# A forward state-space sweep whose rows of prefix sums are requested a quarter earlier, whose two decay products share one tile, and a convolution whose tanh is emitted later

## The chip, the cores and the metric

The kernel runs on one core of one Trainium2 chip. The metric is the device time of one execution, in microseconds (us); the median of three runs before the change is 3792.83 us. The core's engines run side by side, each with its own queue worked off in order: TensorE (PE in the rows, its weight loads PEld), VectorE (DVE), ScalarE (ACT), GpSimd (POOL), and SyncE (SP), which here only issues DMAs.

## The reference

The program is a two-layer network over 256 context and 2048 latent tokens of width 1024, batch 1, float32. The change touches only the even layer's state-space group:

```python
xbc = silu(dwconv(xbc_raw, conv_w, conv_b))        # 5 taps, 1536 channels
xc    = x * dt                                     # 16 heads of 64, chunks of 128 tokens
acum  = cumsum(dt * a)                             # per head, along a chunk
decay = exp(where(lower, acum[l] - acum[s], NEG))  # 128 x 128 per head and direction
y_diag = einsum(C @ B^T, decay, xc)                # within a chunk
y_off  = einsum(C, h_prev, exp(acum))              # from the state before the chunk
```

It is done forwards and backwards over the tokens and both are added. 18 chunks (2 of context, 16 latent) by 16 heads are computed. Attention, gating, an S5 layer and a final norm follow, which the change leaves as they are.

## The kernel before

The even layer's input stage lasts from the start to about 1520 us. TensorE's main work there is the input projection: each weight block of 128 columns is multiplied with "chunks" of 256 tokens, 24 matmuls of 128x128 by 128x256 into one of two PSUM buffers `mm` (float32 split into a high and a low part, three products by eight slices of the contraction). Each filled `mm` must be copied out by ScalarE (or by ScalarE and VectorE together) before TensorE may fill it again. The rows of the sequence are cut into thirds of 768 tokens. For each third, one small block `dt` and 12 convolution blocks run; then the remaining blocks (gate z, q, k, v, g) run for the thirds 2, 1, 0.

A convolution block ends with `conv()`: ScalarE writes the first tap into `cA` (L611, one buffer), VectorE adds four taps in place (L614), ScalarE takes the tanh into `cT` (L617) and VectorE finishes the silu (L618). Twelve units of planned time later `tok()` transposes the block on TensorE (L629, PSUM buffers `tp`, two of them, also used by the dt transposes L804) and ScalarE copies it out (`cE`, L631).

Beside this a second stream, `stream2()`, makes the forward sweep: 18 chunks of 128 tokens by four "quarters" of four heads each. `ssd_fa` does the elementwise part of a quarter and `ssd_fb` its matmuls (`yd`, L964), two quarters behind. In `ssd_fa`, `rf` and `rb` are 128x512 tiles that hold four heads' prefix sums broadcast to all partitions, each loaded by one DMA (L934, L935), two buffers each. ScalarE adds the per-row sum (L942, four instructions), VectorE combines with `rb` (L946, four), ScalarE takes exp (L948). Beside it the product with the masked C B^T of the chunk: ScalarE writes `w1` (L943, four, one buffer) from `cL`, VectorE adds the `cU` part into `w2` (L947, four, three buffers), and L949 multiplies `w2` by `rf`, which is the last read of `rf`. In the rows both tiles are called `w`, since numbers are left out of names.

The code is emitted in an order set by planned time: `merge` steps the main stream, `after(t, f)` calls `f` once the planned clock has passed `t` units, and each quarter of the second stream takes its turn as its share of the budget allows. TensorE executes in just that order. The other engines' instructions, DMA issues of SP among them, are reordered by a scheduler that goes by its own estimates, and are then fixed queues. A tile whose buffer is still in use makes the first instruction that writes it wait.

Of the kernel before, what the change touches and what calls it, by code (L numbers as in the profile page):

```python
# [7 lines left out]
F32 = mybir.dt.float32  # L8
# [3 lines left out]
AF = mybir.ActivationFunctionType  # L12
ALU = mybir.AluOpType
# [3 lines left out]
P = 128  # L17
# [13 lines left out]
AH = 1  # L31
GLD = 16.0
HL = 5.0
RV, KV, QV = 4, 4, 4
GD = 5.0
WGS = 3
# [19 lines left out]
def dap(t, off, dims):  # L56
    return bass.AP(tensor=t.tensor, offset=t.offset + off, ap=[list(d) for d in dims])
# [175 lines left out]
class Net:  # L233
# [220 lines left out]
    def even_in(self):  # L454
        nc, i, tc = self.nc, self.i, self.tc
        with ExitStack() as st:
# [110 lines left out]
            s_dt, s_nP, s_de, s_yo, s_cd = [cp.tile([P, NT, 32], F32, name=n) for n in ("s_dt", "s_P", "s_de", "s_yo", "s_cd")]  # L567
            self.s_dt, self.s_P, self.s_de, self.s_yo, self.s_cd = s_dt, s_nP, s_de, s_yo, s_cd
            self.hst = {0: None, 1: None}

            pj = Proj(self, w_in, 5152, xp, wp, pp)
            thr = lambda th: range(3 * th, 3 * th + 3)
# [6 lines left out]
            def conv_block(th, b):  # L579
# [9 lines left out]
                n = sum(s[1] for s in segs)  # L589
# [15 lines left out]
                def conv():  # L605
# [3 lines left out]
                    acc = vp.tile([P, 896], F32, name="cA", bufs=1)  # L609
                    for (s, m, q) in segs:  # L610
                        nc.scalar.activation(acc[:, q:q + m], R[:, s:s + m], AF.Identity, bias=cbv[:, b:b + 1], scale=cw[:, b:b + 1])  # L611
                    for j in range(1, 5):
                        for (s, m, q) in segs:
                            nc.vector.scalar_tensor_tensor(acc[:, q:q + m], R[:, s + j:s + j + m], cw[:, 12 * j + b:12 * j + b + 1],  # L614
                                                           acc[:, q:q + m], op0=ALU.mult, op1=ALU.add)
                    tg = vq.tile([P, 896], F32, tag="cT", name="cT", bufs=2)
                    nc.scalar.activation(tg[:, :n], acc[:, :n], AF.Tanh)  # L617
                    nc.vector.scalar_tensor_tensor(tg[:, :n], tg[:, :n], 1.0, acc[:, :n], op0=ALU.add, op1=ALU.mult)  # L618
# [14 lines left out]
                        if b == 7:  # L633
                            self.done.add(("xbc", th))
                    if b < 10:
                        self.after(12.0, tok)
                return pj.feat(1024 + b * P, evac, conv, chunks=thr(th))

            def rest_blocks(th):
# [263 lines left out]
    def ssd_off(self, d, c, g, ct, out):  # L903
# [4 lines left out]
        nc.vector.tensor_tensor(out.rearrange("p (h q) -> p h q", h=8), ps.rearrange("p (h q) -> p h q", h=8),  # L908
                                self.s_yo[:, c, h0:h0 + 8][:, :, None].to_broadcast([P, 8, 64]), ALU.mult)

    def ssd_fa(self, c, qq, st):

        nc, sp, pp = self.nc, self.sp, self.pp
        V, G = nc.vector, nc.gpsimd
# [14 lines left out]
        cU, cL = st["c"]  # L929
        g, h0 = qq // 2, qq * 4  # L930
        sh = [P, 4, P]
        rf = sp.tile(sh, F32, name="rf", bufs=2)
        rb = sp.tile(sh, F32, name="rb", bufs=2)
        nc.sync.dma_start(rf, dap(self.prow_d, (c * 32 + h0) * P, [[0, P], [P, 4], [1, P]]))  # L934
        nc.sync.dma_start(rb, dap(self.prow_d, (c * 32 + 16 + h0) * P, [[0, P], [P, 4], [1, P]]))  # L935
        A = nc.scalar
        w1 = sp.tile(sh, F32, name="w1", bufs=1)
        w2 = sp.tile(sh, F32, name="w2", bufs=3)

        for h in range(4):  # L940
            hh = h0 + h
            A.activation(rf[:, h], rf[:, h], AF.Identity, bias=self.s_P[:, c, hh:hh + 1])  # L942
            A.activation(w1[:, h], cL[:, g], AF.Copy, scale=self.s_dt[:, c, 16 + hh:17 + hh])  # L943
        for h in range(4):
            hh = h0 + h
            V.scalar_tensor_tensor(rf[:, h], rb[:, h], self.s_P[:, c, 16 + hh:17 + hh], rf[:, h], op0=ALU.add, op1=ALU.min)  # L946
            V.scalar_tensor_tensor(w2[:, h], cU[:, g], self.s_dt[:, c, hh:hh + 1], w1[:, h], op0=ALU.mult, op1=ALU.add)  # L947
        A.activation(rf, rf, AF.Exp)  # L948
        V.tensor_tensor(w2, w2, rf, ALU.mult)  # L949
        st["w"][qq] = w2  # L950
# [85 lines left out]
    def attention(self):  # L1036
# [4 lines left out]
        with ExitStack() as st:  # L1041
# [268 lines left out]
            def half_proj():  # L1310
                for half in range(2):
# [20 lines left out]
                    if half == 0:  # L1332

                        for _ in range(4):
                            z = ada_load()
                            yield ("until", self.pe + HL)
                            ada_mm(z)
# [862 lines left out]
```

## Time and profile before

| what | value |
|---|---|
| median of 3 runs (lowest to highest) | 3792.83 us (3790.74 to 3793.8) |
| the profiled execution: its time, its span | 3789.91 us, 3788.1 us |
| TensorE busy | 3447.3 us, 91% of the span |
| VectorE, ScalarE, GpSimd busy | 2477.5 us (65%), 1614.5 us (43%), 1146.1 us (30%) |
| mean granted TensorE clock (1 is the full 2.4 GHz) | 0.959 |
| DMA queue 1, share of 16 engines | 63.5% |

TensorE's busy share counts matmuls that overlap in its pipeline; what the other engines cost shows up as idle time before a matmul, and as a lower granted clock after it. The clock has two levels, 2.4 GHz (1.0) and 1.2 GHz (0.5).

### The profile page before, as it was taken

Reading aid. Unit: us, or ns where it says so; the run is one execution under the profiler, and the core shown is the slowest. Engines: PE = TensorE matmul, PEld = TensorE weight load, DVE = VectorE, ACT = ScalarE, POOL = GpSimd, SP = SyncE. Lnnn points to the kernel's source line nnn. Section 1 sums busy time; section 2 is a strip of 40 time slices with the busy share of each in tenths; the row PEclk is TensorE's granted clock in tenths of the full one; section 3 lists DMA queues with packets and bytes.
Section 4 is the critical chain, followed back from the end, with each engine's and each line's share of the span. In section 5 each row is a group of like instructions: output and inputs, shape, how many; then the busy total and the mean of one; then the engine's idle time right before and its main releaser. Section 6 shows DMA issues by size and latency. Waiting matters only on the chain.

```text
span 3788.1 us, 68824 instructions
## 1 busy us (share of the span) xinstructions
PE 3447.3 (91%) x25733; PEld 3100.0 (82%) x25733; DVE 2477.5 (65%) x5414; ACT 1614.5 (43%) x3519; POOL 1146.1 (30%) x754
## 2 busy tenths in 40 slices
PE   6979999998999998789999998978899979989999
PEld 4978898987898888668878887757788978979977
DVE  5878876566535444867677776798893599504355
ACT  4545454443422222667677765222222522343321
POOL 3222234332222332366566652210101111133121
PEclk8989999999999999899999999989899999999999
DMA  8666568775666776675555444557877854895453
GB/s 287 219 212 197 176 216 267 251 233 194 218 233 207 261 253 211 188 195 148 147 138 136 117 115 131 163 171 230 256 239 244 295 185 147 272 299 163 126 167 112
DMA packets 668025, 759.33 MB, mean 200 GB/s; under 512 B 77147, under 2 KB 529691, under 8 KB 667691
## 3 DMA queue, kind: packets, MB, share of 16 engines
q1 hardware_dynamic: 667691, 754.93, 63.5%
q8 instruction: 203, 3.33, 0.4%
q14 instruction: 131, 1.07, 0.1%
HBM read 517.62 MB, written 237.15 MB: 199 GB/s over the span
## 4 chain that ended last, share of the span: by engine, by line
PE 30%; DVE 13%; DMA 7%; SPq 2%; issue 2%; ACT 2%; POOL 1%; DVEq 0%; ACTq 0%; POOLq 0%
PE pv L1184 3%; PE pt L1174 3%; PE S L1154 2%; PE mm L289 2%; PE gpo L291 2%; PE gpo L290 2%; PE gpo L289 2%; PE S L1156 2%; PE mm L290 2%; PE mm L291 2%; DVE sc L1896 1%; PE f L289 1%; PE f L291 1%; PE f L290 1%; DVE sc L1899 1%
## 5 line engine op out<-in xcount | busy, mean ns | idle before, releaser
L289 PE MATMUL mm<-xTh,wh 128*128 128x256 f32 (+1 forms) x3320 | 1014.8, 306 | 68.9 <-ACT cR L603 22.4
L290 PE MATMUL mm<-xTl,wh 128*128 128x256 f32 (+1 forms) x3320 | 956.6, 288 | 1.3 <-POOL xTl L274 0.7
L291 PE MATMUL mm<-xTh,wl 128*128 128x256 f32 (+1 forms) x3320 | 955.8, 288 | 0.5 <-DVE wl L274 0.5
L289 PEld LDWEIGHTS mm<-xTh,wh 128*128 128x128 f32 (+1 forms) x3320 | 648.6, 195 | 100.9 <-ACT cR L603 24.8
L290 PEld LDWEIGHTS mm<-xTl,wh 128*128 128x128 f32 (+1 forms) x3320 | 648.6, 195 | 18.2 <-issue 14.9
L291 PEld LDWEIGHTS mm<-xTh,wl 128*128 128x128 f32 (+1 forms) x3320 | 646.8, 195 | 1.7 <-DVE wl L274 0.8
L1178 DVE TENSOR_TENSOR tl<-pt,th 128x512 fp32r<-128x512 f32 x328 | 224.2, 687 | 117.6 <-ACT th L1177 115.1
L1167 DVE TENSOR_SCALAR_CACHE_REDUCE p<-S,nsink 128x640 f32<-128x640 f32 (+2 forms) x288 | 235.3, 820 | 79.4 <-PE S L1156 76.6
L1168 ACT ACTIVATE p<-p,nm 128x640 f32<-128x640 f32 (+2 forms) x288 | 223.9, 777 | 69.9 <-DVE p L1167 67.8
L1177 ACT ACTIVATE th<-pt 128x512 fp32r<-128x512 f32 x328 | 194.2, 593 | 132.0 <-PE pt L1174 128.6
L289 PE MATMUL mm<-wh,xTh 128*128 128x256 f32 x720 | 217.9, 303 | 20.0 <-DMA wh<-wk 10.6
L1174 PE MATMUL pt<-ident,p 128*128 128x128 f32 x1312 | 203.4, 277 | 33.4 <-ACT p L1168 14.2
L1174 PEld LDWEIGHTS pt<-ident,p 128*128 128x128 f32 x1312 | 156.1, 141 | 68.4 <-issue 18.7
L290 PE MATMUL mm<-wl,xTh 128*128 128x256 f32 x720 | 206.7, 287 | 1.7 <-POOL wl L274 1.0
L291 PE MATMUL mm<-wh,xTl 128*128 128x256 f32 x720 | 206.3, 287 | 0.0
L946 DVE SCALAR_TENSOR_TENSOR rf<-rb,s_P,rf 128x128 f32<-128x128 f32 x288 | 135.0, 514 | 97.8 <-ACT rf L942 92.1
L614 DVE SCALAR_TENSOR_TENSOR cA<-cR,vecs,cA 128x256 f32<-128x256 f32 (+3 forms) x192 | 182.6, 962 | 23.6 <-ACT cA L611 20.2
L401 POOL TENSOR_TENSOR xin<-xin,shr 128x1024 f32<-128x1024 f32 x33 | 86.3, 2625 | 313.3 <-issue 185.4
L289 PEld LDWEIGHTS mm<-wh,xTh 128*128 128x128 f32 x720 | 140.9, 196 | 27.6 <-DMA wh<-wk 11.4
L274 POOL TENSOR_TENSOR wl<-w,wh 128x1024 fp32r<-128x1024 f32 (+1 forms) x43 | 100.4, 2338 | 199.7 <-ACT wh L282 177.8
L576 ACT ACTIVATE tz<-mm 128x256 f32<-128x256 f32 x144 | 54.0, 378 | 232.4 <-PE mm L291 229.9
L408 PE MATMUL tp<-ident,xin 128*128 128x128 f32 x432 | 93.9, 304 | 63.7 <-DVE xTl L274 44.8
(458 smaller groups left out, 9011.7 us busy)
## 6 DMA issues: line engine op xcount, KB each, us to landing
wh<-wk SPq DMA_DIRECT2D x116, 512.0 KB
wl<-wk SPq DMA_DIRECT2D x116, 512.0 KB
wk<-wh SPq DMA_DIRECT2D x56, 512.0 KB
wk<-wl SPq DMA_DIRECT2D x56, 512.0 KB
w<-in_e_w_in_dram SPq DMA_DIRECT2D x40, 512.0 KB
xin<-in_x_dram SPq DMA_DIRECT2D x38, 512.0 KB
rf<-prow_d SPq DMA_DIRECT2D x72, 256.0 KB
rb<-prow_d SPq DMA_DIRECT2D x72, 256.0 KB
```

The source lines that it names most:

```text
L274: eng.tensor_tensor(out, x, hi.bitcast(F32), ALU.subtract)
L289: mm(ps, lhsT=ah, rhs=bh, start=first, stop=False)
L290: mm(ps, lhsT=ah, rhs=bl, start=False, stop=False)
L291: mm(ps, lhsT=al, rhs=bh, start=False, stop=last)
L614: nc.vector.scalar_tensor_tensor(acc[:, q:q + m], R[:, s + j:s + j + m], cw[:, 12 * j + b:12 * j + b + 1], acc[:, q:q + m], op0=ALU.mult, ...
L946: V.scalar_tensor_tensor(rf[:, h], rb[:, h], self.s_P[:, c, 16 + hh:17 + hh], rf[:, h], op0=ALU.add, op1=ALU.min)
L1167: V.tensor_scalar(p[:, :w], s, -0.125, nsink[:, h:h + 1], op0=ALU.mult, op1=ALU.min, accum_out=nm)
L1168: A.activation(p[:, :w], p[:, :w], AF.Exp, bias=nm, scale=-1.0, accum_out=d["sm"][:, h:h + 1])
L1174: T.transpose(pt[:, n, :], Ps[h4][:, j * P:(j + 1) * P], self.ident)
L1177: A.activation(th, pt, AF.Copy)
L1178: V.tensor_tensor(tl, pt, th.bitcast(F32), ALU.subtract)
L1184: T.matmul(pv, lhsT=VV[kt][:, hk, :], rhs=t.rearrange("p a b -> p (a b)"), start=first and x == 0, stop=last and x == 1)
```

## The change

Three edits. First, `ssd_rows` issues both row loads of a quarter; `ssd_fa` calls it for the next quarter at the start of the present one (not across the ends of the three thirds' sweeps, where it loads its own rows as before). The tiles keep two buffers. Second, `w1` is gone: ScalarE writes its product into `w2`, VectorE adds to it in place, and `w2` has four buffers in place of three. Third, tanh and all that follows of a convolution block are called `CVT` = 4 planned units after the taps; the transposes keep 12 units from the block's end in the text of the plan.

```diff
+CVT = 4.0
@@ conv() of conv_block
                             nc.vector.scalar_tensor_tensor(acc[:, q:q + m], R[:, s + j:s + j + m], cw[:, 12 * j + b:12 * j + b + 1],
                                                            acc[:, q:q + m], op0=ALU.mult, op1=ALU.add)
+                    self.after(CVT, lambda: silu(acc))
+
+                def silu(acc):
                     tg = vq.tile([P, 896], F32, tag="cT", name="cT", bufs=2)
...
                     if b < 10:
-                        self.after(12.0, tok)
+                        self.after(12.0 - CVT, tok)
@@ class Net
+    def ssd_rows(self, c, qq):
+
+        r = [self.sp.tile([P, 4, P], F32, name=n, bufs=2) for n in ("rf", "rb")]
+        for d in range(2):
+            self.nc.sync.dma_start(r[d], dap(self.prow_d, (c * 32 + 16 * d + qq * 4) * P, [[0, P], [P, 4], [1, P]]))
+        return r
@@ ssd_fa
-        rf = sp.tile(sh, F32, name="rf", bufs=2)
-        rb = sp.tile(sh, F32, name="rb", bufs=2)
-        nc.sync.dma_start(rf, dap(self.prow_d, (c * 32 + h0) * P, [[0, P], [P, 4], [1, P]]))
-        nc.sync.dma_start(rb, dap(self.prow_d, (c * 32 + 16 + h0) * P, [[0, P], [P, 4], [1, P]]))
+        rf, rb = self.rows_q.pop((c, qq), None) or self.ssd_rows(c, qq)
+        if (c, qq) not in ((4, 3), (10, 3), (17, 3)):
+
+            n = (c, qq + 1) if qq < 3 else (c + 1, 0)
+            self.rows_q[n] = self.ssd_rows(*n)
         A = nc.scalar
-        w1 = sp.tile(sh, F32, name="w1", bufs=1)
-        w2 = sp.tile(sh, F32, name="w2", bufs=3)
+        w2 = sp.tile(sh, F32, name="w2", bufs=4)
 
         for h in range(4):
             hh = h0 + h
             A.activation(rf[:, h], rf[:, h], AF.Identity, bias=self.s_P[:, c, hh:hh + 1])
-            A.activation(w1[:, h], cL[:, g], AF.Copy, scale=self.s_dt[:, c, 16 + hh:17 + hh])
+            A.activation(w2[:, h], cL[:, g], AF.Copy, scale=self.s_dt[:, c, 16 + hh:17 + hh])
         for h in range(4):
             hh = h0 + h
             V.scalar_tensor_tensor(rf[:, h], rb[:, h], self.s_P[:, c, 16 + hh:17 + hh], rf[:, h], op0=ALU.add, op1=ALU.min)
-            V.scalar_tensor_tensor(w2[:, h], cU[:, g], self.s_dt[:, c, hh:hh + 1], w1[:, h], op0=ALU.mult, op1=ALU.add)
+            V.scalar_tensor_tensor(w2[:, h], cU[:, g], self.s_dt[:, c, hh:hh + 1], w2[:, h], op0=ALU.mult, op1=ALU.add)
```

The order changes on all engines up to the end of the forward sweep and is the same behind it. Line numbers of the changed kernel are higher: L603, L611, L617, L631, L813, L942, L943, L948 become L605, L613, L622, L636, L818, L954, L955, L960, and both row loads stand in L920.

ScalarE at the first chunk of the second third's blocks, where the sweep's first products are made. `cR` are copies out of `mm`, `d_e` belongs to the dt block; the kernel before:

```order
L603 ACTIVATE cR<-mm 128x256
L943 ACTIVATE w_2423<-cL,s_dt 128x128 x4
L611 ACTIVATE cA<-cR,vecs 128x768
L813 ACTIVATE d_e<-d_e 128x192
L943 ACTIVATE w_2570<-cL,s_dt 128x128 x4
L603 ACTIVATE cR<-mm 128x256 x2
L942 ACTIVATE rf<-rf,s_P 128x128 x4
```

and the changed kernel:

```order
L605 ACTIVATE cR<-mm 128x256 x3
L636 ACTIVATE cE<-tp 128x512
L613 ACTIVATE cA<-cR,vecs 128x768
L636 ACTIVATE cE<-tp 128x128
L818 ACTIVATE d_e<-d_e 128x192
L955 ACTIVATE w_2453<-cL,s_dt 128x128 x4
L955 ACTIVATE w_2612<-cL,s_dt 128x128 x4
L955 ACTIVATE w_2814<-cL,s_dt 128x128 x4
L955 ACTIVATE w_2992<-cL,s_dt 128x128 x4
L605 ACTIVATE cR<-mm 128x256 x3
```

The products of all four quarters now stand in one piece behind `d_e` and ahead of the copies; before, those of the second quarter did, and the third and fourth came later.

ScalarE at the first chunk of the last third's blocks, again products, copies and the row lines; before:

```order
L943 ACTIVATE w_4099<-cL,s_dt 128x128 x4
L690 ACTIVATE dT<-mm 32x256
L943 ACTIVATE w_4338<-cL,s_dt 128x128 x4
L943 ACTIVATE w_4512<-cL,s_dt 128x128 x4
L603 ACTIVATE cR<-mm 128x256
L942 ACTIVATE rf<-rf,s_P 128x128 x8
L603 ACTIVATE cR<-mm 128x256
L948 ACTIVATE rf<-rf 128x512
L631 ACTIVATE cE<-tp 128x512
```

and the changed kernel:

```order
L955 ACTIVATE w_4121<-cL,s_dt 128x128 x4
L955 ACTIVATE w_4359<-cL,s_dt 128x128 x4
L955 ACTIVATE w_4532<-cL,s_dt 128x128 x4
L605 ACTIVATE cR<-mm 128x256
L954 ACTIVATE rf<-rf,s_P 128x128
L605 ACTIVATE cR<-mm 128x256
L954 ACTIVATE rf<-rf,s_P 128x128 x3
L818 ACTIVATE d_e<-d_e 128x192
L954 ACTIVATE rf<-rf,s_P 128x128 x4
L960 ACTIVATE rf<-rf 128x512
L605 ACTIVATE cR<-mm 128x256
L636 ACTIVATE cE<-tp 128x512
```

The products keep their place; the second copy moved ahead of three quarters of the row lines. On TensorE the dt transposes L804, which stood right behind a block's transposes L629, now stand one chunk of 24 matmuls ahead of them.

SP in the gate blocks of the second third, one chunk of the sweep; `wk` are weights read back for a later block, `xs`, `ct`, `bt` the sweep's other loads; before:

```order
L934 DMA rf<-prow_d 128x512 x2
L868 DMA xs<-xs_d 128x1024
L648 DMA z_d<-zt 128x2x256
L870 DMA ct<-ct_d 128x2x128
L872 DMA bt<-btok_d 128x256
L935 DMA rb<-prow_d 128x512 x2
L934 DMA rf<-prow_d 128x512
L976 DMA yp_d<-y 128x1024
L648 DMA z_d<-zt 128x2x256
L935 DMA rb<-prow_d 128x512
L934 DMA rf<-prow_d 128x512
L82 DMA wl<-wk_2720_01_7100 128x1024
```

and the changed kernel:

```order
L920 DMA rf<-prow_d 128x512 x2
L873 DMA xs<-xs_d 128x1024
L653 DMA z_d<-zt 128x2x256
L875 DMA ct<-ct_d 128x2x128
L877 DMA bt<-btok_d 128x256
L920 DMA rb<-prow_d 128x512
L988 DMA yp_d<-y 128x1024
L920 DMA rb<-prow_d 128x512
L920 DMA rf<-prow_d 128x512 x2
L653 DMA z_d<-zt 128x2x256
L920 DMA rb<-prow_d 128x512 x2
L83 DMA wh<-wk_2720_00_7075 128x1024
```

The four `rf` loads stand at the same count ahead of the weights, and one more `rb` does. Over the whole sweep no weight load has its count of `rf` or `rb` loads ahead of it changed by more than two of 72, and most by none.

## Rows read from the trace of the kernel before

**Rows 1.** Busy time by engine, 60 to 560 us; then granted clock, DMA share, GB/s

```profile
60.00:560.00 500.00, 447.12 (x3530) 429.12 (x3530) 414.69 (x639) 244.50 (x546) 139.26 (x91) 0.95 0.64 206
```

**Rows 2.** What TensorE waited for, 60 to 1120 us: total, times, longest

```profile
PE mm L289 <- ACT cR L603: 22.4, 8, 9.6
...
PE mm L289 <- DVE zt L577: 11.6, 7, 2.7
PE mm L289 <- DMA wh<-wk: 9.1, 2, 4.7
PE tp L804 <- ACT cE L631: 8.4, 2, 7.8
PE mm L289 <- DVE qev L577: 8.3, 3, 4.1
```

**Rows 3.** Groups by line, 60 to 1110 us: busy, mean ns | idle before, releasers

```profile
L943 ACT ACTIVATE w<-cL,s_dt 128x128 f32<-128x128 f32 x288 | 92.6, 391 | 77.2 <-DVE w L947 53.6 <-DVE cL L924 23.1
L942 ACT ACTIVATE rf<-rf,s_P 128x128 f32<-128x128 f32 x288 | 92.3, 391 | 109.3 <-DMA rf<-prow_d 108.7
...
L617 ACT ACTIVATE cT<-cA 128x640 f32<-128x640 f32 (+2 forms) x36 | 30.3, 843 | 52.2 <-DVE cA L614 48.3 <-DMA prow_d<-rows 4.0
...
L947 DVE SCALAR_TENSOR_TENSOR w<-cU,s_dt,w 128x128 f32<-128x128 f32 x288 | 113.9, 448 | 15.5 <-PE yd L964 9.2 <-ACT w L943 6.3
```

**Rows 4.** Timeline, 231 to 243 us: start, length, engine, line, [idle before, releaser]

```profile
231.55 0.35 ACT L813 ACTIVATE d_e<-d_e 128x192 f32<-128x192 f32 x1
...
233.19 1.91 POOL L926 TENSOR_TENSOR y<-xs,dskip 128x1024 f32<-128x1024 f32 x1
...
233.27 7.70 DVE L947 SCALAR_TENSOR_TENSOR w<-cU,s_dt,w 128x128 f32<-128x128 f32 x4
...
241.01 1.28 ACT L943 ACTIVATE w<-cL,s_dt 128x128 f32<-128x128 f32 x4 [9.11 <-DVE w L947]
...
242.60 0.58 PE L289 MATMUL mm<-xTh,wh 128*128 128x256 f32 x1 [9.59 <-ACT cR L603]
```

**Rows 5.** Timeline, 381 to 395 us, ScalarE and TensorE

```profile
381.31 1.28 ACT L943 ACTIVATE w<-cL,s_dt 128x128 f32<-128x128 f32 x4 [5.71 <-DVE cL L924]
...
385.89 0.82 PE L629 MATMUL tp<-ident,cT 128*128 128x128 f32 x6
...
388.94 0.36 ACT L603 ACTIVATE cR<-mm 128x256 f32<-128x256 f32 x1
389.71 1.28 ACT L942 ACTIVATE rf<-rf,s_P 128x128 f32<-128x128 f32 x4 [0.42 <-DMA rf<-prow_d]
391.93 1.28 ACT L942 ACTIVATE rf<-rf,s_P 128x128 f32<-128x128 f32 x4 [0.94 <-DMA rf<-prow_d]
...
394.53 0.84 PE L804 MATMUL tp<-ident,dT 32*128 32x32 f32 x6 [7.82 <-ACT cE L631]
```

**Rows 6.** Timeline, 95 to 97 us, ScalarE and TensorE

```profile
95.29 0.74 ACT L617 ACTIVATE cT<-cA 128x640 f32<-128x640 f32 x1 [11.05 <-DVE cA L614]
...
96.36 0.58 PE L289 MATMUL mm<-xTh,wh 128*128 128x256 f32 x1 [7.17 <-ACT cR L603]
```

**Rows 7.** Busy time and clock in three short stretches (columns as Rows 1)

```profile
242.00:245.60 3.60, 3.00 (x14) 3.00 (x15) 3.60 (x7) 1.42 (x5) 0.00 (x0) 0.50 0.24 73
245.60:249.20 3.60, 3.60 (x32) 3.60 (x32) 3.60 (x11) 2.49 (x9) 0.00 (x0) 1.00 0.28 71
...
389.00:399.20 10.20, 4.67 (x24) 4.61 (x25) 5.90 (x16) 5.27 (x16) 0.00 (x0) 0.50 0.40 120
```

**Rows 8.** Timeline, 821 to 827 us: a row buffer's last read, its load, its next use

```profile
821.61 1.41 DVE L949 TENSOR_TENSOR w<-w,rf 128x512 f32<-128x512 f32 x1
...
823.08 0.32 SPq L934 DMA_DIRECT2D rf<-prow_d  x1
...
826.52 1.28 ACT L942 ACTIVATE rf<-rf,s_P 128x128 f32<-128x128 f32 x4 [3.05 <-DMA rf<-prow_d]
```

**Rows 9.** What SP's queue waited for, 170 to 1110 us: total, times, longest

```profile
SPq L934 <- DVE w L949: 59.0, 36, 12.1
```

More of the change, by code (lines that the diff above doesn't have):

```diff
@@ L569, in even_in @@
             self.hst = {0: None, 1: None}
+            self.rows_q = {}
             pj = Proj(self, w_in, 5152, xp, wp, pp)
```

## The prediction

> **What bounds the kernel now.** I first read the order of before and after, which says where to look: only the stretch up to the end of the forward sweep changes, and TensorE's instructions there are the same ones. What can move the time is therefore TensorE's idle time in that stretch and the clock it loses by it. Busy time by stage shows TensorE at 447.12 of 500 us and VectorE not far behind at 414.69 [rows 1]. TensorE's waits say what ends its idle time: mostly a copy out of PSUM that comes late, by ScalarE (`cR` 22.4 us in 8 waits, `cE` 8.4) or by ScalarE and VectorE together (`zt` 11.6, `qev` 8.3), and twice a weight load (9.1) [rows 2]. Two of these waits are nearly half of it: 9.59 us at 242.6 and 7.82 us at 394.5; a third is 7.17 us at 96.4 [rows 4 to 6]. Why ScalarE is late then stands in its groups by line: it sits idle in front of the row lines for DMA (108.7 us), in front of the products for VectorE's use of the single `w1` (53.6 us), and in front of the tanh for the taps (48.3 us) [rows 3]. The three edits aim at one of these each. Idle time of ScalarE costs only where a copy that TensorE needs stands behind it, so I price the edits by TensorE's stalls.
>
> A stall also costs clock. After the 9.59 us the granted clock is 0.50 for 3.6 us, in which 14 matmuls pass; in the next 3.6 us, at 1.00, 32 do [rows 7]. So one matmul takes 3.6 / 32 = 0.1125 us at the full rate, a chunk of 24 takes 2.7 us, and work done at the low level costs half its time extra.
>
> **The products (`w1` gone, fourth buffer).** At 241.01 ScalarE starts the second quarter's products after 9.11 us of waiting for VectorE, whose four L947 took 7.70 us; the copies of `mm` stand behind, and TensorE waits 9.59 us [rows 4]. In the new order 16 products stand behind `d_e` and need no VectorE. `d_e` ends at 231.55 + 0.35 = 231.90. Four products take 1.28 us at 0.391 each, so a further one adds (1.28 - 0.39) / 3 = 0.297 us, and 16 take 0.39 + 15 x 0.297 = 4.8 us. The copy, 0.36 us, ends at about 237.1 in place of 242.6. TensorE had run dry at 242.60 - 9.59 = 233.0, so about 4.1 us of idle stays and 5.5 us go. The low clock stays as long as a wait of that size does; I count none back. Bounds: nothing, if `cL` or the taps hold the copies anyway, and 9.6 + 1.5 us if all of it goes.
>
> At 394.5 TensorE has been dry since 394.53 - 7.82 = 386.7. Twelve products from 381.31 on take 3.7 us, so the first copy comes at 385.0 in place of 388.94 [rows 5], and the dt transposes, which waited for a PSUM buffer of the transposes just ahead, stand a chunk earlier. TensorE gets one chunk, 2.7 us, to 389.4; the second copy then stands behind one row line, whose DMA lands at 389.71, and comes by 390.5 (1.1 us idle); the third stands behind the other row lines, 391.93 + 1.28, an exp and itself, about 394.2, against a chunk that ends at 393.2 (1.0 us idle). Of 7.8 us some 2.1 stay and 5.7 go, and of the 4.67 us of work at the low level [rows 7], which costs 2.3 us, I take half back: 6.9 us. Bounds 0 and 7.8 + 2.3 = 10.1.
>
> The fourth buffer ends VectorE's 9.2 us of waiting for `yd` before L947 [rows 3]. That reaches TensorE only where a `zt` or `qev` stands behind it: between 0 and 9.2 us, I take 1, since VectorE's other delays stay.
>
> **The tanh.** It is called two chunks later, but the queue's order shows that the scheduler had already put one or two `cR` copies ahead of it; now it is mostly two. At 95.3 the taps ended late (11.05 us of waiting), one copy more now stands ahead, and TensorE gets one more chunk before it is dry: 2.7 of 7.17 us [rows 6]. The other `cR` waits are 22.4 - 9.59 - 7.17 = 5.6 us together; I take 1. Bounds 0 and 7.2 + 5.6 + 2.9 us of clock. The transposes go one chunk later, and the code behind them has room: no TensorE wait in rows 2 is for a sweep load.
>
> **The rows a quarter ahead.** I take nothing, and this is the choice that decides the sum. ScalarE's 108.7 us look like loads asked for too late. But a row load waits for its buffer and not for its turn: at 821.61 + 1.41 = 823.02 the last read of an `rf` buffer ends, at 823.08 SP issues the load of the quarter two later into it, and 3.4 us after that ScalarE uses it, having waited 3.05 [rows 8]. SP waited for that reader 36 times, 59.0 us [rows 9]. The queue already runs ahead as far as two buffers let it; the change keeps two buffers, and the order of SP shows the loads at almost the same count among the weight loads. Bounds: the stalls a late row can have held, `zt` and `qev`, 11.6 + 8.3 = 19.9 us saved; and 9.1 us lost if the one `rb` more ahead of some weight loads makes the two waits for weights as long again.
>
> **The sum.** 5.5 + 6.9 + 1 + 2.7 + 1 + 0 = 17.1 us. TensorE's gained time brings work to VectorE faster, and that is 83% busy in the convolution stage (414.69 of 500); I give 3 us back for stalls that come up elsewhere. That leaves 14 us: the profiled execution, 3789.91 us, would take 3776, and the median, which lies 2.9 us above it, 3792.83 - 14 = 3779.
>
> **Rivals.**
>
> *The early rows do help.* For it: 108.7 us of DMA waiting is the largest sum on ScalarE. Against it: rows 8 and 9. It would add most of the 19.9 us: about 3779 - 18 = 3761. 13%.
>
> *VectorE takes the place of the wait.* Without ScalarE's wait the four L947 still take 7.70 us, where four at the mean of 0.448 would take 1.8; GpSimd's multiplies of 1.9 us run beside them [rows 3, 4]. Everything behind them, taps, exp's inputs, `zt`, is as late as before, and with `cA` in one buffer the copies of `cR` soon wait for the taps. Then only the 2.7 us of the tanh stay: about 3790, range 3785 to 3797. For it speaks the 83%, against it that VectorE also idles in front of these lines. 27%. The Trainium skill, page "SBUF — State Buffer", section "SBUF: two separate sides", has a rule for the long L947: a VectorE operation with two SBUF inputs and a GpSimd operation that reads SBUF take a shared port pair as an exclusive lock for a whole instruction. By that rule the in-place add, which still has two SBUF inputs, is held as before, and this rival's time would hold; the trace agrees as to the length (7.70 us beside 1.91 us multiplies), not yet as to the time.
>
> *Slower: bursts of products.* Twelve products now run as one piece of 3.7 us at each of 18 chunks; with the copy, 4.0 us. TensorE has one other `mm` buffer, 2.7 us of work. If both are full when the burst begins, each chunk costs 1.3 us, 23 us in all, less the 14: about 3802. It decides if the burst meets a full buffer at most chunks. Against it: before, the same products with their waits held ScalarE longer, and TensorE was stalled much by them only twice. 10%.
>
> **How the numbers follow.** My forecast, 3779 with its own range 3770 to 3786, gets 46%; the rivals 13, 27 and 10; 4% is for none of these, near 3786. For 8 in 10 the range reaches into the first two, 3760 to 3797; what is left out is most of the slower case and half of the first. Runs of this kernel differ by about 0.2%, 7.6 us, so faster means below 3785.2 and slower above 3800.4. Faster: 0.43 of the forecast, 0.13, and a fifth of the second, 0.06, and 0.02: 0.64. Slower: 0.07 of the burst case, 0.02 of the second and 0.01: 0.10. The rest, 0.26, is the same.
>
> **What would show it.** Right: the products' wait for VectorE (53.6 us) gone; the stall near 242.6 about 4 us and that at 394.5 about 2; the row lines still waiting 80 to 120 us for DMA; their loads still issued within 0.1 us of the buffer's last read. Wrong: a DMA wait below 50 us (first rival); TensorE's waits for VectorE and for `cR` higher by what the two stalls lost (second); a wait of 1 to 2 us behind products at each chunk (third); a change behind the sweep, where the order is the same.

## The result and the profile after

The changed kernel takes 3821.08 us (median of 4 runs, 3815.74 to 3825.94) against 3793.32 us for the kernel before on the same chip: a ratio of 1.0078, 95% interval [1.0061, 1.0094]. It is slower by 28 us in the medians and by 30 us by the ratio, where 14 us of gain were forecast. The profiled execution took 3815.74 us.

Some words for what follows. An *eviction* is the copy of a filled `mm` out of PSUM. In the later blocks ScalarE makes the half `tz` of it and VectorE then the half `zt` or `qev`. The *combines* are VectorE's four instructions that join `rf` and `rb` (L946 before, L958 changed), the *closing multiply* is the product of `w2` and `rf` (L949, L961).

Where the time went is read from the two stretches of the forward sweep. Up to 530 us the convolution blocks run beside it, from there on the z, q, k, v, g blocks. Busy time by stretch (columns as in Rows 1), first the kernel before:

```profile
60.00:530.00 470.00, 419.83 (x3318) 403.50 (x3318) 390.75 (x603) 232.82 (x519) 124.15 (x84) 0.95 0.63 202
530.00:1140.00 610.00, 568.16 (x4301) 534.18 (x4300) 345.37 (x696) 248.88 (x668) 196.22 (x102) 0.97 0.69 233
```

and the changed kernel:

```profile
60.00:530.00 470.00, 422.62 (x3317) 405.31 (x3316) 391.06 (x601) 227.88 (x509) 126.33 (x84) 0.96 0.64 202
530.00:1140.00 610.00, 549.17 (x4084) 515.14 (x4083) 351.22 (x686) 245.56 (x668) 188.78 (x98) 0.94 0.67 222
```

In the first stretch TensorE's idle time falls by 2.8 us (50.2 to 47.4). In the second it rises by 19.0 us (41.8 to 60.8), and the granted clock falls from 0.97 to 0.94: 12 intervals at the low level with 51.5 us of matmul work in place of 9 with 32.8, so 18.7 us more work at half rate, 9.4 us of time. Together that is 28.4 us. Set side by side by the count of projection matmuls, the two executions lie 2.9 us apart in the changed kernel's favour at the 2880th (534.2 and 531.3 us), and 28.4 us in the other direction at the 6000th (1070.4 and 1098.7). So they part by 31.3 us between these two matmuls, of which idle time and clock explain 28.4; behind the sweep the distance stays within 25 to 30 us.

What TensorE waited for in the changed kernel, 60 to 1140 us (total, times, longest), answers [rows 2]:

```profile
PE mm L290 <- ACT cR L605: 30.8, 12, 6.7
PE mm L290 <- DVE zt L579: 14.5, 4, 6.4
PE mm L290 <- ACT qev L665: 13.8, 6, 3.6
PE mm L290 <- DVE qev L579: 12.4, 2, 7.5
```

The waits for `cR` have grown by 8.4 us, more than the 3.4 us by which all those for `cE` fell (10.6 to 7.2). Of the evictions of the later blocks, those that ScalarE makes alone (`qev`, L665) grew most, from 2.8 us in 2 waits to 13.8 in 6; those that VectorE ends come in fewer and longer waits, up to 7.5 us where the longest was 4.1. ScalarE's groups in the changed kernel, 60 to 1140 us, against [rows 3]:

```profile
L954 ACT ACTIVATE rf<-rf,s_P 128x128 f32<-128x128 f32 x288 | 92.2, 390 | 105.7 <-DMA rf<-prow_d 105.6
L955 ACT ACTIVATE w<-cL,s_dt 128x128 f32<-128x128 f32 x288 | 88.0, 389 | 17.1 <-DVE cL L936 16.3 <-PE yd L976 0.8
L960 ACT ACTIVATE rf<-rf 128x512 f32<-128x512 f32 x72 | 44.8, 626 | 85.3 <-DVE rf L958 84.5
```

So the edit did what it says: the 53.6 us in which the products waited for VectorE are gone. The row lines' wait for DMA is hardly touched (108.7 to 105.6). The exp now waits 84.5 us for VectorE's combines (64.0 before), and the longest of the new stalls stand behind the same combines.

**The longest stall, 841.5 us.** Timeline of the changed kernel (start, length, engine, line; in brackets idle time and releaser):

```profile
827.04 1.23 DVE L958 SCALAR_TENSOR_TENSOR rf<-rb,s_P,rf 128x128 f32<-128x128 f32 x4 [1.27 <-ACT rf L954]
...
832.42 0.68 DVE L961 TENSOR_TENSOR w<-w,rf 128x512 f32<-128x512 f32 x1
832.64 2.22 POOL L892 TENSOR_TENSOR h<-h,s_cd 128x1024 f32<-128x1024 f32 x1 [0.89 <-DVE h L904]
...
833.16 8.00 DVE L958 SCALAR_TENSOR_TENSOR rf<-rb,s_P,rf 128x128 f32<-128x128 f32 x4
...
834.82 1.95 POOL L883 TENSOR_TENSOR xw<-xs,s_de 128x1024 f32<-128x1024 f32 x1
834.85 0.36 ACT L578 ACTIVATE tz<-mm 128x256 f32<-128x256 f32 x1
836.73 2.38 POOL L275 TENSOR_TENSOR wl<-w,wh 128x1024 fp32r<-128x1024 f32 x1
839.07 1.94 POOL L938 TENSOR_TENSOR y<-xs,dskip 128x1024 f32<-128x1024 f32 x1
841.08 0.41 DVE L579 SCALAR_TENSOR_TENSOR qev<-tz,mm 128x256 f32<-128x256 f32 x1
...
841.55 0.58 PE L290 MATMUL mm<-xTh,wh 128*128 128x256 f32 x1 [7.49 <-DVE qev L579]
```

ScalarE has its half of the eviction, `tz`, done at 835.2. VectorE's half, `qev`, takes 0.41 us, but the four combines of the next quarter stand ahead of it in the queue. They take 8.00 us (four with no GpSimd instruction beside them took 1.23 us at 827.04), and in those 8 us GpSimd runs four whole-width instructions without a gap; one combine gets through for each: taken one by one in the trace, the combines end at 835.00, 836.91, 839.25 and 841.16, each about 0.15 us behind the end of a GpSimd instruction. The kernel before had the same place too, with 4.63 us of combines and a stall of 3.69:

```profile
826.96 4.63 DVE L946 SCALAR_TENSOR_TENSOR rf<-rb,s_P,rf 128x128 f32<-128x128 f32 x4 [3.03 <-ACT rf L942]
...
832.50 0.43 PE L289 MATMUL mm<-xTh,wh 128*128 128x256 f32 x1 [3.69 <-DVE qev L577]
```

**The stall at 989.2 us** shows the same with GpSimd's order moved by the change:

```profile
979.62 1.34 POOL L982 TENSOR_TENSOR y<-y,yt 128x512 f32<-128x512 f32 x1 [16.76 <-DVE yt L913]
...
980.73 0.37 ACT L578 ACTIVATE tz<-mm 128x256 f32<-128x256 f32 x1
980.92 1.95 POOL L883 TENSOR_TENSOR xw<-xs,s_de 128x1024 f32<-128x1024 f32 x1
...
983.76 1.90 POOL L892 TENSOR_TENSOR h<-h,s_cd 128x1024 f32<-128x1024 f32 x1 [0.89 <-DVE h L904]
983.80 4.43 DVE L958 SCALAR_TENSOR_TENSOR rf<-rb,s_P,rf 128x128 f32<-128x128 f32 x4
985.62 1.95 POOL L938 TENSOR_TENSOR y<-xs,dskip 128x1024 f32<-128x1024 f32 x1
988.16 0.68 DVE L961 TENSOR_TENSOR w<-w,rf 128x512 f32<-128x512 f32 x1
988.76 0.41 DVE L579 SCALAR_TENSOR_TENSOR zt<-tz,mm 128x256 f32<-128x256 f32 x1
...
989.22 0.58 PE L290 MATMUL mm<-wh,xTh 128*128 128x256 f32 x1 [6.42 <-DVE zt L579]
```

In the kernel before, `xw` of that chunk came first, as soon as its tile had landed:

```profile
963.80 1.91 POOL L878 TENSOR_TENSOR xw<-xs,s_de 128x1024 f32<-128x1024 f32 x1 [16.61 <-DMA xs<-xs_d]
...
965.66 1.35 POOL L970 TENSOR_TENSOR y<-y,yt 128x512 f32<-128x512 f32 x1
...
969.27 0.39 PE L289 MATMUL mm<-wh,xTh 128*128 128x256 f32 x1 [1.37 <-DVE zt L577]
```

### The profile page after: what moved, and what is told of

Same layout as the page of the kernel before. It is cut to its first block, busy times and chain, and to the rows that moved or that the text cites. A ratio compares the mean times of both kernels' runs of the same rounds, so it can differ in the third digit from the quotient of the medians.

```text
span 3813.9 us, 68826 instructions
## 1 busy us (share of the span) xinstructions
PE 3459.7 (91%) x25733; PEld 3109.5 (82%) x25733; DVE 2487.8 (65%) x5414; ACT 1609.1 (42%) x3519; POOL 1149.4 (30%) x754
## 4 chain that ended last, share of the span: by engine, by line
PE 29%; DVE 14%; DMA 7%; SPq 2%; issue 2%; ACT 2%; POOL 1%; DVEq 0%; ACTq 0%; POOLq 0%
PE pv L1196 3%; PE pt L1186 3%; PE S L1166 2%; PE mm L290 2%; PE gpo L292 1%; PE mm L291 1%; PE mm L292 1%; PE S L1168 1%; DVE Bu L1913 1%; PE gpo L291 1%; PE gpo L290 1%; DVE sc L1908 1%; DMA oo<-o_d 1%; PE f L290 1%; PE f L291 1%
## 5 line engine op out<-in xcount | busy, mean ns | idle before, releaser
L290 PE MATMUL mm<-wh,xTh 128*128 128x256 f32 x720 | 221.2, 307 | 21.5 <-DVE zt L579 14.5
L616 DVE SCALAR_TENSOR_TENSOR cA<-cR,vecs,cA 128x256 f32<-128x256 f32 (+3 forms) x192 | 181.0, 954 | 21.8 <-ACT cA L613 18.4
L958 DVE SCALAR_TENSOR_TENSOR rf<-rb,s_P,rf 128x128 f32<-128x128 f32 x288 | 137.9, 526 | 78.9 <-ACT rf L954 77.4
L291 PEld LDWEIGHTS mm<-wl,xTh 128*128 128x128 f32 x720 | 143.1, 199 | 12.7 <-POOL wl L275 6.2
```

The source lines that it names most:

```text
L290: mm(ps, lhsT=ah, rhs=bh, start=first, stop=False)
L291: mm(ps, lhsT=ah, rhs=bl, start=False, stop=False)
```

## The experiments

Theories at the start: **A**, GpSimd's three whole-width multiplies of each chunk (`xw`, the decay of `h`, `dskip`), moved into one piece, hold VectorE's combines and with them the evictions; **B**, first that the later tanh does it, then (from the fifth run on) that evictions queue behind row lines that wait for their loads, GpSimd or not; **C**, the rows loaded ahead do it. **D** was set down for the runs on the fourth buffer with the multiplies on VectorE: the fourth buffer of `w2` lets VectorE's queue put combines and closing multiplies ahead of evictions. Ratios are to the kernel before on the same chip; 0.1% is 3.8 us. A ratio of two such ratios has its interval from both, taken as independent.

### One part at a time

The product in place with four buffers, alone:

```diff
-        w1 = sp.tile(sh, F32, name="w1", bufs=1)
-        w2 = sp.tile(sh, F32, name="w2", bufs=3)
+        w2 = sp.tile(sh, F32, name="w2", bufs=4)
...
-            A.activation(w1[:, h], cL[:, g], AF.Copy, ...)
+            A.activation(w2[:, h], cL[:, g], AF.Copy, ...)
```

> Only the second part of the change: w1 is gone, the product is written in place into w2, which has four buffers; rows loaded as before and tanh as before. Theory A (the scheduler answers this edit by sending GpSimd's multiplies xw, h and dskip in one piece, and VectorE's row combines of 2.0 to 2.4 us beside them stop TensorE): slow, about +18 to +28 us (3811 to 3821), nearly all of it between 530 and 1100 us, with stalls of TensorE of 5 to 7 us there. Theory B (the later tanh moves TensorE's own order and that costs the time): within 5 us of before. Theory C (the rows loaded ahead cost it): within 5 us of before.

Measured: 1.0043 [1.0028, 1.0058]. Slow, as A says and B and C don't, but with 16 us only about half the loss.

The later tanh alone (`+ self.after(CVT, lambda: silu(acc))`, and 12.0 - CVT for the transposes):

> Only the third part: the tanh of a convolution block is emitted 4.0 later in the plan. Theory A: about -3 to +3 us against before (3790 to 3796), since GpSimd's order in the later chunks stays that of before. Theory B: slow, about +20 to +28 us (3813 to 3821). Theory C: within 5 us of before.

Measured: 1.0015 [1.0001, 1.0030], about 6 us slower, so B in its first form falls. The trace shows a gain that is handed back: TensorE's idle time between 60 and 530 us is 46.6 us against 50.2, between 530 and 1140 us 45.0 against 41.8.

The rows a quarter ahead alone (`rf, rb = self.rows_q.pop(...)` and the call of `ssd_rows` for the next quarter):

> Only the first part: the rows of prefix sums are asked for a quarter ahead. Theories A and B: within 3 us of before (3790 to 3796), as the engines' order is that of before but for seven lines of the queue that issues the loads, and the buffer still comes free only when its last reader is done. Theory C: +15 us or more.

Measured: 0.9991 [0.9979, 1.0003], no difference. C falls.

The changed kernel without the rows ahead (its two `dma_start` back where they were):

> The changed kernel with the rows loaded where the kernel before loads them; the product in place and the later tanh stay. Theories A and B: as slow as the changed kernel, +22 to +32 us (3815 to 3825). Theory C: the loss is gone, within 5 us of before.

Measured: 1.0057 [1.0036, 1.0077]. Against the changed kernel that is 1.0021 ± 0.0026: whether the rows cost something beside the other two parts stays open; at least 14 us of the loss are there without them.

The product in place with three buffers (`name="w2", bufs=3`):

> As the run with the product in place alone, but with three buffers of w2 as before instead of four: the difference is what the fourth buffer does. Theories A and B: within 5 us of the run with four (3799 to 3809). Rival: the fourth buffer lets the products run further ahead and that moved GpSimd's order; then most of the loss goes, 3786 to 3794.

Measured: 1.0014 [0.9999, 1.0028]. The time is the rival's: the fourth buffer alone is 1.0029 ± 0.0021, 11 us. Its reason, GpSimd's order, is not: the late `xw` and its stall are here too (5.39 us at 977.1). And the product in place without the buffer brings none of the 12.4 us that the prediction had for it. Its trace shows why, at the first of the two places. ScalarE and TensorE, 248 to 250 us:

```profile
248.40 1.28 ACT L950 ACTIVATE rf<-rf,s_P 128x128 f32<-128x128 f32 x4 [11.60 <-DMA rf<-prow_d]
249.59 0.36 ACT L605 ACTIVATE cR<-mm 128x256 f32<-128x256 f32 x1
250.00 0.58 PE L290 MATMUL mm<-xTh,wh 128*128 128x256 f32 x1 [7.50 <-ACT cR L605]
```

The copy no longer stands behind a product that waits 9.11 us for VectorE [rows 4]; it stands behind a row line that waits 11.60 us for its load, whose buffer came free only at 243.7 us, behind the same slow VectorE work. At the second place (392.7 us) 6.22 of the 7.82 us are left, behind a row line that waits 5.8 us. Over the whole sweep the row lines' wait for DMA rises from 108.7 to 133.2 us, and VectorE's L955 waits 24.1 us for ScalarE's products (6.3 us in [rows 3]):

```profile
  DMA rf<-prow_d: 133.2, 45
```

The changed kernel with three buffers of `w2`:

> The changed kernel with three buffers of w2 instead of four, all else as changed. If the fourth buffer's cost stands by itself as it did with the product alone (11 us): 3800 to 3809 in the scale of before at 3788. If it is only one of many ways in which the order falls: as the changed kernel, 3812 to 3822.

Measured: 1.0023 [1.0005, 1.0041], 3797 us, below the bounds of both answers: the fourth buffer costs more here than with the product alone. One number is changed against the changed kernel, and 1.0055 ± 0.0024 of its 1.0078 are gone. TensorE's order is the same in both. At the place of the longest stall the evictions now come first:

```profile
822.00 0.68 DVE L961 TENSOR_TENSOR w<-w,rf 128x512 f32<-128x512 f32 x1
822.19 2.25 POOL L883 TENSOR_TENSOR xw<-xs,s_de 128x1024 f32<-128x1024 f32 x1 [0.86 <-DVE h L904]
822.60 0.41 DVE L579 SCALAR_TENSOR_TENSOR qev<-tz,mm 128x256 f32<-128x256 f32 x1
...
824.24 0.42 DVE L579 SCALAR_TENSOR_TENSOR qev<-tz,mm 128x256 f32<-128x256 f32 x1 [1.23 <-ACT tz L578]
...
827.24 4.03 DVE L958 SCALAR_TENSOR_TENSOR rf<-rb,s_P,rf 128x128 f32<-128x128 f32 x4 [2.58 <-ACT rf L954]
...
833.43 0.38 PE L290 MATMUL mm<-xTh,wh 128*128 128x256 f32 x1 [3.01 <-DVE qev L579]
```

Two `qev` run between the closing multiply and the combines, and the stall is 3.01 us in place of 7.49. The stall near 989 stays (7.61 us at 980.0 here), as it does in every run with the product in place and GpSimd's multiplies.

### GpSimd's multiplies

Both kernels without the three multiplies:

```diff
     def ssd_xw(self, d, c, xs):
+        if d == 0:
+            return xs
...
-        if old is not None:
+        if old is not None and d:
...
-            G.tensor_tensor(y..., xs..., self.dskip..., ALU.mult)
...
-            nc.vector.tensor_tensor(y[:, gs], y[:, gs], py..., ALU.add)
+            nc.vector.tensor_tensor(y[:, gs], xs[:, gs], py..., ALU.add)
```

> The kernel before, with GpSimd's three whole-width multiplies of the forward sweep left out (xw, the decay of h, dskip): xs stands in for xw and for the skip term, the state is summed without decay; VectorE, ScalarE and TensorE keep every instruction. It is the base for the next run. Theory A (GpSimd's multiplies in one piece hold VectorE's combines): the row combines fall from a mean of about 510 ns to about 360 ns, and the time falls by 10 to 20 us (3768 to 3778). Theory B (what stops TensorE is that tz and qev queue on ScalarE and VectorE behind a row line that waits for its load): within 6 us of before.

> The changed kernel with the same three multiplies left out. Theory A: with GpSimd out of the way the changed kernel is as fast as the run beside it or faster: 0 to 14 us below it, as the prediction had it. Theory B: the loss stays, 15 to 30 us above the run beside it.

Measured: 0.9911 [0.9888, 0.9934] and 0.9929 [0.9910, 0.9949]. The multiplies cost the kernel before 34 us and the changed kernel 56 us, and without them the changed one is 1.0018 ± 0.0030 of the other: the loss needs the multiplies. Nothing of the forecast gain comes out either. The kernel before gained more than A had it (34 us, not 10 to 20), while its combines fell from a mean of 514 ns to 404 and not to 360 (60 to 1110 us).

The same work on VectorE, none left out:

```diff
-        nc.gpsimd.tensor_tensor(xw..., ALU.mult)
+        (nc.gpsimd if d else nc.vector).tensor_tensor(xw..., ALU.mult)
... (the decay of h and dskip likewise)
```

> The kernel before with GpSimd's three whole-width multiplies of the forward sweep (xw, the decay of h, dskip) done by VectorE instead: the same products, the same waits for them, none left out. VectorE gets some 54 instructions of about 1.4 us (twice a 128x512 row of 0.68 us), 74 us in all. Theory A1 (what the multiplies cost is that VectorE's short combines stand beside them and take 2 us each): faster than before by 5 to 25 us (3762 to 3782), and the row combines fall to a mean of about 360 ns. Theory A2 (what they cost is that the state and y wait for their results): no gain, 0 to +20 us (3787 to 3807).

> The changed kernel with the same three multiplies on VectorE. Theory A1: within 8 us of the run beside it, so most of the loss of 30 us is gone. Theory A2: the loss stays, 15 to 35 us above the run beside it.

Measured: 0.9932 [0.9906, 0.9958] for the kernel before, 3763 us; 1.0017 [1.0003, 1.0031] for the changed one, 1.0086 ± 0.0030 of the run beside it. So A1 holds for what the multiplies cost, in both kernels (26 and 23 us come back), and fails for the loss: all of it is still there, though these multiplies no longer run on GpSimd beside the combines. VectorE's combines of the kernel before, 530 to 1110 us, before and after the move (busy, mean ns | idle before, releaser):

```profile
L946 DVE SCALAR_TENSOR_TENSOR rf<-rb,s_P,rf 128x128 f32<-128x128 f32 x211 | 109.6, 565 | 81.9 <-ACT rf L942 81.8
```

```profile
L946 DVE SCALAR_TENSOR_TENSOR rf<-rb,s_P,rf 128x128 f32<-128x128 f32 x208 | 81.4, 436 | 55.6 <-ACT rf L942 55.5
...
L878 DVE TENSOR_TENSOR xw<-xs,s_de 128x1024 f32<-128x1024 f32 x13 | 17.9, 1380 | 7.5 <-DMA xs<-xs_d 7.5
```

The mean falls by 129 ns, to 436 and not to the 360 that was expected; `wl` and the sums into `y` stay on GpSimd. A multiply takes 1.2 to 1.4 us on VectorE, while on GpSimd it took about 2 us and could hold a combine as long. TensorE gets the difference (530 to 1140 us, columns as in Rows 1; idle 33.6 us in place of 41.8, clock 0.99 in place of 0.97):

```profile
530.00:1140.00 610.00, 576.40 (x4417) 540.57 (x4416) 365.22 (x744) 250.86 (x672) 118.51 (x63) 0.99 0.72 238
```

Then the fourth buffer, with the multiplies on VectorE and without them:

> The changed kernel with the three multiplies on VectorE and three buffers of w2 instead of four. Theory D (with a fourth buffer VectorE takes the combine and the closing multiply of the next quarter ahead of the evictions TensorE waits for): most of the 34 us go, 3763 to 3778 (0.993 to 0.997 of before), and the time that evictions between 530 and 1110 us stand on VectorE after ScalarE is done with its half falls from 78 us to 66 or less. Rival (the product in place or the later tanh do it): within 8 us of the changed kernel with its multiplies on VectorE, 3788 to 3804.

Measured: 0.9964 [0.9950, 0.9978]. The fourth buffer costs 1.0053 ± 0.0020, 20 us, with none of the three multiplies on GpSimd: the time came as D had it. The sum D went by did not: between 530 and 1110 us, the time from the end of `tz` to the start of VectorE's half, added over the evictions, fell from 77.7 to 75.8 us only (in the two pairs with the multiplies on GpSimd it fell by 18.4 and 10.3 us). It is no measure of the loss by itself (65.2 us in the fastest of these kernels, 56.9 in the kernel before); a sum over the times when TensorE stood idle is given under "What is shown and what is not".

> The changed kernel with the three multiplies left out and three buffers of w2. If the fourth buffer costs only where a long instruction stands in VectorE's queue ahead of an eviction: within 6 us of the same with four buffers (0.9929 of before), 0.991 to 0.9945. If it costs whatever stands there: 11 to 21 us faster than with four, 0.987 to 0.990.

Measured: 0.9918 [0.9893, 0.9943], against 0.9929 with four buffers: 1.0011 ± 0.0032, no difference that could be measured. The fourth buffer costs 11 to 21 us where the multiplies run, on either engine. Where they don't, a cost of 20 us is excluded, one of 11 us is not.

> The kernel before with the product in place, three buffers of w2 and the multiplies on VectorE; tanh and rows as before. If the product in place holds the 12 us: 0.995 to 0.998 of before. If it is free once the multiplies are on VectorE: within 5 us of the kernel before with them there (0.9932), 0.992 to 0.9945. If the wait it takes away was worth what the prediction said: 0.989 to 0.991.

Measured: 0.9969 [0.9955, 0.9983], 1.0037 ± 0.0029 of the kernel before with its multiplies on VectorE. By the medians the product in place holds the 12 us that were left, so with the multiplies on VectorE it costs where it was meant to save; but the interval reaches from 3 to 25 us, and the two profiled executions differ by under 1 us (3767.26 and 3766.41).

> Only the later tanh, with the three multiplies on VectorE. Theory T1 (its 11 us of TensorE's idle time saved in the convolution were handed back to GpSimd's multiplies later): faster than the kernel before with its multiplies on VectorE by 4 to 12 us, 0.990 to 0.992 of before. Theory T2 (they are handed back whatever GpSimd does, since the sweep's steps come later on TensorE): within 4 us of it or slower, 0.992 to 0.996.

Measured: 0.9925 [0.9898, 0.9952], 0.9993 ± 0.0037 of the kernel without the later tanh: T2's bounds, but the interval doesn't exclude T1. With the multiplies on VectorE the later tanh neither costs nor brings anything that could be measured.

> The kernel before with xw and the decay of h on VectorE and dskip on GpSimd. If the price of the multiplies is that they come in one piece: one multiply alone holds one or two combines a chunk, and this is as fast as all three on VectorE, 0.990 to 0.995 of before. If each multiply has its own price: about a third of the gain is missing, 0.995 to 0.997.

Measured: 0.9954 [0.9936, 0.9971], two thirds of the gain (17 of 26 us) with two of three multiplies moved. That is what a price of its own for each would give; by the interval (1.0022 ± 0.0031 of all three moved) it is not told apart from the other answer.

### Rows that are really early

Three buffers of `rf`, three of `w2` for the room:

```diff
-        r = [self.sp.tile([P, 4, P], F32, name=n, bufs=2) for n in ("rf", "rb")]
+        r = [self.sp.tile([P, 4, P], F32, name=n, bufs=b) for n, b in (("rf", 3), ("rb", 2))]
...
-        w2 = sp.tile(sh, F32, name="w2", bufs=4)
+        w2 = sp.tile(sh, F32, name="w2", bufs=3)
```

> The changed kernel with three buffers of rf instead of two, so that the load a quarter ahead has a free buffer, and three of w2 to make the room. TensorE's order is the changed kernel's own. Theory A: ScalarE's row lines wait less for loads (from 81 us to under 30 between 60 and 1110 us) but the time stays within 8 us of the changed kernel (3807 to 3825), as the combines still meet GpSimd's pieces. Theory B: the loss goes with the wait, 3775 to 3795.

Measured: 1.0047 [1.0031, 1.0064], and the row lines wait 134.6 us for loads, more than in the changed kernel (105.6): neither theory's wait came true, so it decided nothing. (The 81 us that the expectation starts from is no wait for loads in that trace.) Two numbers are changed here; the run with one of them, three buffers of `w2`, waits 146.0 us and takes 1.0023, so the third buffer of `rf` takes nothing off the time (1.0024 ± 0.0025). Then both row tiles with three buffers, `w2` with two, and the same with the multiplies on VectorE:

> The changed kernel with three buffers of rf and of rb and two of w2. If the row loads are what ScalarE waits for in place of VectorE: its wait for them falls from 106 us to under 40 between 60 and 1110 us, and the time comes below the changed kernel with three buffers of w2 (1.0023 of before), 0.992 to 1.000. If the rows' wait covers nothing that TensorE needs: the wait falls and the time stays at 1.000 to 1.004. If two buffers of w2 are too few: 1.005 or more.

> The same with the three multiplies on VectorE, a candidate for the fastest. If early rows help: below the kernel before with its multiplies on VectorE, 0.985 to 0.992 of before. If they don't: 0.993 to 0.998, as the run with three buffers of w2 (0.9964).

Measured: 1.0059 [1.0038, 1.0081] and 1.0039 [1.0023, 1.0054]. What the row lines waited for in the first of them:

```profile
  DMA rf<-prow_d: 210.6, 65
```

Neither run came as forecast for early rows. The wait doubles, and the first time is the one that stood for two buffers of `w2` being too few (1.005 or more); the second lies above all its bounds. Each load is still issued as soon as the buffer's last reader is done (quarter 10: the multiply of quarter 7 ends at 358.4 us, the load goes out at 358.4, and ScalarE uses it from 361.5, after 3.9 us of idle time). Why the wait grows is not shown, since the rows got a buffer more and `w2` two fewer at once. In the other runs with the product in place it is 105.6 to 145.6 us with four buffers of `w2` and 115.8 to 146.8 with three, one of these with three of `rf` (134.6), so the two buffers of `w2` are as likely a cause as the rows' third. A run with three buffers of the rows and four of `w2` was not made.

## Why the prediction was wrong

**The step that failed first is the fourth buffer.** The prediction asked how much of VectorE's 9.2 us of waiting for `yd` reaches TensorE, "between 0 and 9.2 us", and took 1 us of gain. The wait did go (60 to 1110 us, against [rows 3]):

```profile
L959 DVE SCALAR_TENSOR_TENSOR w<-cU,s_dt,w 128x128 f32<-128x128 f32 x288 | 122.5, 481 | 6.1 <-ACT w L955 6.1
```

But the bounds left out a loss, with no reason given, and a loss it was: 11 us with the product alone, 21 us in the changed kernel, 20 us with the multiplies on VectorE. At the longest stall the scheduler put evictions ahead of the next quarter's combines with three buffers, and the combines ahead of `qev` with four. Without the fourth buffer the rest of the change is 9 us slower than before (1.0023), where the other terms, give-back included, promised 13 us of gain: they failed too, as follows.

**The products, 12.4 us of gain.** The mechanism of the working held where it was read: 16 products take 4.78 us (4.8 predicted) and the copy comes right behind them. Of the changed kernel, 231 to 252 us:

```profile
231.44 4.78 ACT L955 ACTIVATE w<-cL,s_dt 128x128 f32<-128x128 f32 x16 [0.30 <-DVE cL L936]
236.13 0.63 ACT L605 ACTIVATE cR<-mm 128x256 f32<-128x256 f32 x2
...
236.54 0.58 PE L290 MATMUL mm<-xTh,wh 128*128 128x256 f32 x1 [6.16 <-ACT cR L605]
...
250.47 0.84 ACT L622 ACTIVATE cT<-cA 128x768 f32<-128x768 f32 x1 [8.55 <-DVE cA L616]
251.22 0.37 ACT L605 ACTIVATE cR<-mm 128x256 f32<-128x256 f32 x1
...
251.64 0.58 PE L290 MATMUL mm<-xTh,wh 128*128 128x256 f32 x1 [4.39 <-ACT cR L605]
```

The copies end at 236.8, near the 237.1 predicted. But TensorE had run dry at 230.4 and not at 233.0, so 6.16 us stay and not 4.1, and a second stall of 4.39 us follows, in which the copy stands behind a tanh that waits 8.55 us for the taps. VectorE's work beside GpSimd was as late as before, and the wait went to the next line that needs it. (Two waits that the prediction calls nearly half of what ends TensorE's idle time, 9.59 and 7.82 us, are a third of the 52.9 us idle in [rows 1]; no term hangs on that.) Near 394.5 the stall fell to 1.28 and 1.73 us (2.1 predicted), and 3.85 us came up at 414.2. The give-back was put at 3 us for the whole sweep; in this stretch alone it took nearly everything: of the 14.9 us of idle time that the terms took out here (5.5, 5.7, 2.7 and 1), 2.8 us came. With three buffers the product in place alone gains nothing (1.0014).

**The tanh, 3.7 us of gain.** At 96.2 us 6.68 of 7.17 us stay, where 4.5 were predicted. One copy more does stand ahead of the tanh now, but it waits itself for the same taps, which still read `cR`:

```profile
95.75 0.39 ACT L605 ACTIVATE cR<-mm 128x256 f32<-128x256 f32 x1 [11.19 <-DVE cA L616]
```

So the term had the order right and the wait wrong. The 3.6 us of idle time that the part saves in the convolution stretch are handed back behind it.

**The rows, nothing.** Right, by the reason given: the wait is 105.6 us within the forecast 80 to 120, the part alone measures 0.9991, most `rf` loads (54 of 70) go out within 0.1 us of the end of a closing multiply, and the queue still waits for the buffer's last reader (SP's waits, 170 to 1110 us, against [rows 9]):

```profile
SPq L920 <- DVE w L961: 55.0, 31, 5.1
```

The first rival, early rows, falls for this change by the same wait, which it had below 50 us. What a shorter wait would bring stays open: no run with more buffers for the rows had one.

**The place.** All terms of the sum but the 1 us of the fourth buffer lie before 530 us, since there the longest stalls were. The loss arose behind it, where the prediction has nothing but that 1 us. The second rival named the right waits (TensorE's for VectorE and for `cR` higher) but its price ended at 3797; the slower rival had the right sign and the wrong mechanism: of the 18 bursts of 12 or 16 products only the first, at 231 us, is followed within 2 us by a wait for a copy of more than 0.5 us.

**The long combines.** Four combines take 8.00 us beside four GpSimd instructions and 1.23 us without, and moving the multiplies away gave 26 us. The Trainium skill, page "SBUF — State Buffer", section "SBUF: two separate sides", says that a VectorE operation with two SBUF inputs and a GpSimd operation that reads SBUF share a port pair that one of them locks for an instruction. The trace agrees: one combine gets through for each GpSimd instruction. The prediction priced no stall of the second stretch with those 2 us a combine, though four combines of 4.63 us stood there in the trace of before.

**What is shown and what is not.** Shown by pairs of runs: the loss needs the three multiplies, on whichever engine; the fourth buffer is most of it; the rows alone are free. The 9 us that are left are the product in place and the later tanh, not told apart beside GpSimd's multiplies (1.0014 and 1.0015 alone).

How the fourth buffer costs time was read above from the longest stalls. A sum over all of them bears it out. Between the 2880th and the 6000th projection matmul, the combines that VectorE was running while TensorE stood idle for a `zt` or `qev` add up to 7.8 us in the kernel before, 20.4 in the changed one and 11.9 with three buffers; 19.9 and 12.1 with the product alone; 9.3 and 4.2 with the multiplies on VectorE; 5.2 and 3.5 without them. All combines together take 135.0 us before and 137.9 in the changed kernel: they are not longer, they stand ahead of evictions that TensorE needs. By the 6000th matmul the fourth buffer has cost 14.5, 4.8, 11.2 and -0.6 us in these four pairs of profiled executions. The rest of the medians' 21, 11 and 20 us is not located; behind that matmul single executions of all these kernels differ by up to 20 us.

Why the product in place moves `xw` behind the second of a chunk's two sums into `y` (L970, L982) is the scheduler's choice and was not tried apart.

**A faster version.** The kernel before with its three multiplies on VectorE takes 3763 us, 0.9932 of before, with the later tanh 3758 (0.9925 [0.9898, 0.9952]); between the two the runs do not tell.

## What to carry to other kernels

A wait taken from an in-order queue moves everything behind it forward: before counting the gain, read which instruction now stands ahead of the one that TensorE needs, in every stretch and on every engine, not only at the longest stalls of before. A deeper buffer can cost time, because a full buffer holds back work that nobody needs yet; give its bound on the side of loss as well. Where short VectorE instructions with two SBUF inputs run beside whole-width GpSimd ones, look in the trace whether only one gets through per GpSimd instruction, as here, price them so, and try the wide ones on VectorE.

## What the runs showed of the hardware

Four 128x128 combines of VectorE take 1.23 us undisturbed and 8.00 us beside four GpSimd instructions of 1.94 to 2.38 us, so one for each. The same 128x1024 multiply takes 1.91 us on GpSimd and 1.21 us on VectorE (medians), and with 53 of them moved, 3788 us become 3763.
